# Interleaving two tokens instead of four in the one-hot matrices of a gate product

## The chip, the cores and the metric

The kernel runs on one core of one Trainium2 chip. The metric is the device time of one execution in microseconds (us). The profile tells of five engines: PE (TensorE, matrix products; PEld is its weight load, which runs beside the products), DVE (VectorE), ACT (ScalarE), POOL (GpSimd) and SP (SyncE, which here only issues DMAs).

## What is computed

The reference runs two transformer layers one after the other over 512 tokens of width 1024. The change lies in the last step of the second layer, a product-key mixture of experts ("PEER"): each token picks, in each of 8 heads, 16 of 128 x 128 experts, gives each pick a softmax weight, and sums the picked rows.

```python
idx = jnp.take_along_axis(cand_i, pos, axis=-1)          # i1 * 128 + i2
g = jax.nn.softmax(top_s, axis=-1)
u = down[idx]
act = jax.nn.gelu(jnp.einsum("thkd,td->thk", u, xb).astype(F32), approximate=False)
return jnp.einsum("thk,thkd->td", (g * act).astype(xb.dtype), up[idx])
```

## The kernel before

Each of the 512 tokens has 128 picks (8 heads x 16), each a pair of numbers (i1, i2) and a weight g. The first 128 tokens fetch their expert rows one by one (`gen_fetch`). For the other 384 the kernel takes all 16384 experts densely: scores of every expert for every token (`s_mm`, two halves of 12 matmuls with 384 columns for each of 128 expert blocks), times a gate matrix G[i1, i2] per token that holds the summed weight of each picked expert and zero elsewhere.

The gate matrices are what the change touches. `decode(a)` works out i1, i2 and g of a block of 128 tokens, transposes them on PE so that the partitions are the 128 picks, and stores them in the table `hk_` (i2, i1, the f16 high part of g, the f16 rest of g; four rows of 128 tokens). `gates(a, hook)` then walks over the 128 tokens in groups q of four, two groups at a time, so 16 iterations for each of the blocks a = 1, 2, 3, 48 in all, and 96 groups. For each group DVE makes two instructions of 1024 f16 elements: an equality test of the table against 0..127 (`iota4`), which gives the one-hot rows of i2 and i1 (`oh`), and a product of the i1 one-hot with the two parts of g (`gh`). `gates_mm` then makes 8 matmuls for the group: for each of its 4 tokens, the one-hot of i2 is the stationary and the weighted one-hot of i1 the moving operand, 128 x 128 x 128, once for each part of g, into one PSUM bank. So there are 96 x 8 = 768 such gate matmuls, and 192 such DVE instructions.

Within a group the four tokens are interleaved: element (i, token r) of a one-hot lies at 4 * i + r, so that a token's 128 elements, which a matmul reads, lie four f16 elements, 8 bytes, apart, for both operands.

The order is written out by hand. An iteration issues on DVE: test, test, product, product of two groups. Then `gates_flush` issues the ACT instructions that move the finished banks out (`gates_out`: 512 elements into `b_Gs`, and after eight groups a DMA to `gscr` and two POOL copies), `gates_mm` issues the 16 matmuls of the pair of groups made one iteration before, and `hook` (`ghook`) issues one half of an expert score (`sp(1)`: 12 matmuls, `s_mm`), pending weight-split work on DVE and ACT, and in iterations 5 to 9 one fetched row on DVE. The one-hot buffers are four (`b_oh`, turned by `ohr`), so DVE can be two pairs of groups ahead of PE. Scores are made ahead for 56 of the 128 expert blocks (`NPRE`): what is not made beside the gates is made right after them, and then comes the main loop of `NGR * KT` = 128 steps, to the end of the kernel.

Of the kernel before, what the change touches and what calls it, by code (L numbers as in the profile page):

```python
# [13 lines left out]
ALU = mybir.AluOpType  # L14
AX = mybir.AxisListType.X
MUL, ADD, SUB = ALU.mult, ALU.add, ALU.subtract

P = 128
# [3 lines left out]
NT = 4  # L22
# [10 lines left out]
GW = 32768.0  # L33
# [184 lines left out]
def build(tc, A, cst, coff, uoff, out, stop=None, dbg=None):  # L218
# [8 lines left out]
    V, S, G, PE, SP = nc.vector, nc.scalar, nc.gpsimd, nc.tensor, nc.sync  # L227
# [5 lines left out]
    def al(n, top=False):  # L233
        n = max(8, -(-n // 8) * 8)
        for i in (range(len(holes) - 1, -1, -1) if top else range(len(holes))):
            o, m = holes[i]
            if m >= n:
                if top:
                    holes[i] = (o, m - n)
                    b = Buf(arena[:, o + m - n:o + m], o + m - n, n)  # L240
                else:
                    holes[i] = (o + n, m - n)
                    b = Buf(arena[:, o:o + n], o, n)
                if holes[i][1] == 0:
                    holes.pop(i)
                return b
        raise MemoryError(f"arena: {n} wanted, {holes}")
# [30 lines left out]
    def mm(o, l, r, start=True, stop=True):  # L278
        PE.matmul(o, l, r, start=start, stop=stop)  # L279

    def tr(o, i):
        PE.transpose(o, i, (ident if i.dtype == F32 else ident16)[:i.shape[0], :i.shape[0]])  # L282
# [9 lines left out]
    def act(o, i, f=AF.Copy, **kw):  # L292
        S.activation(o, i, f, **kw)  # L293
# [10 lines left out]
    def stt(o, a, s, b, op0, op1):  # L304
        V.scalar_tensor_tensor(o, a, s, b, op0=op0, op1=op1)  # L305

    def tt(o, a, b, op, e=None):
        (e or V).tensor_tensor(o, a, b, op=op)  # L308
# [81 lines left out]
    def need(key):  # L390
        while key not in ready:
            before = len(ready)
            pump_split(1)
            assert len(ready) > before, (key, q_split[:3], len(spl_free), len(stg_free), list(staged))
        return ready[key]
# [31 lines left out]
    def wk(b, nk, ncol, c0, n=P):  # L427
        h, l = b.h(nk, ncol), b.h(nk, ncol, at=2048)
        return [(h[:, k, c0:c0 + n], l[:, k, c0:c0 + n]) for k in range(nk)]
# [3 lines left out]
    ident, ones, iota = small(P), small(P), small(P)  # L433
# [543 lines left out]
    for a in range(2):  # L977
        b = tbk()
# [7 lines left out]
    for a in range(NT):  # L986
        b, b2 = tbk(), tbk()
# [442 lines left out]
    for a, _ in enumerate(tokproj("rv", hx, range(NT), to_act(rv))):  # L1430
# [4 lines left out]
        else:  # L1435
            d = a - 2
            b = sb_()
# [64 lines left out]
    b = sb_()  # L1502
# [8 lines left out]
    for i in range(2):  # L1511
        b = tb()
# [6 lines left out]
    for i in range(6):  # L1519
        b = lbk()  # L1520
# [75 lines left out]
    w = need(("in", 8))  # L1596
    for p in range(2):
        b = pb()
# [170 lines left out]
    for n in range(KT):  # L1769
        w = wk(need(("wout", n // 2)), KT, 256, P * (n % 2))  # L1770
        b = pb()
# [100 lines left out]
    def sp(n=1):  # L1872
        for _ in range(n):
            if se[2] < NPRE:
                pieces[se[3] % 2]()
                se[3] += 1
# [62 lines left out]
    for h in range(8):  # L1939
        w = need(("wq", h))  # L1940
# [27 lines left out]
        for aa in range(2):  # L1968
            b = gbk()
# [29 lines left out]

    b_g, b_i, b_if = al(NT * P), al(NT * P), al(NV // 2)  # L2000
    gw, i12, If = b_g.f(NT, 16, 8), b_i.h(2, NT, P), b_if.h(NT, 2, 16, 8)
    b_mx, b_pf, b_ij, b_i4 = al(NT * 8), [al(256) for _ in range(4)], al(1024), al(256)
    mx = b_mx.f(NT * 8)
    ts_ = b_TS.f(NT * 8, 16)
    pos, pa, pb_, pt_ = (b.h(NT * P) for b in b_pf)
    iotaj, iota4 = b_ij.h(16, P), b_i4.h(P, 4)
    G.tensor_copy(iotaj, iota[:, 0:16].unsqueeze(2).to_broadcast([P, 16, P]))
    G.tensor_copy(iota4, iota.unsqueeze(2).to_broadcast([P, P, 4]))
    V.tensor_copy(pos.rearrange("p (a k h) -> p a k h", a=NT, k=16), PO.rearrange("p a h k -> p a k h"))
    V.tensor_copy(mx, ts_[:, :, 0])  # L2010
    tt(ts_, ts_, mx.unsqueeze(2).to_broadcast([P, NT * 8, 16]), SUB)
# [24 lines left out]
    b_eq, b_ix, b_hk = al(1024), al(P + EX), [al(4 * 64) for _ in range(2)]  # L2036
# [4 lines left out]
    def decode(a):  # L2041
        for i, ps_ in enumerate((pa, pb_)):
            x_ = ps_[:, P * a:P * a + P].unsqueeze(1)
            tt(eq, iotaj, x_.to_broadcast([P, 16, P]), ALU.is_equal)
            sp(PRE[2])
            eq4 = b_eq.h(16, 16, 8)
            tt(eq4, eq4, If[:, a, i].unsqueeze(2).to_broadcast([P, 16, 16, 8]), MUL)
            for n in (8, 4, 2):
                tt(eq[:, 0:n], eq[:, 0:n], eq[:, n:2 * n], ADD)
            sp(PRE[2])  # L2050
            tt(i12[:, i, a], eq[:, 0], eq[:, 1], ADD)
        if a < 2:
            t = tmps[a][:, 0:P]
            stt(t, i12[:, 0, a], 128.0, i12[:, 1, a], MUL, ADD)
            V.tensor_copy(ix[0] if a == 0 else ix1, t)
        if a:
            hk_ = b_hk[a % 2].h(4, P)
            b = gbk()
            b16 = b.bitcast(F16)
            for i in range(2):  # L2060
                tr(b16[:, P * i:P * i + P], i12[:, 1 - i, a])
            tr(b[:, 256:256 + P], gw[:, a].rearrange("p k h -> p (k h)"))
            act(hk_[:, 0:2], b16[:, 0:256].rearrange("p (i t) -> p i t", i=2))
            act(hk_[:, 2], b[:, 256:256 + P], scale=GW)
            stt(hk_[:, 3], b[:, 256:256 + P], GW, hk_[:, 2], MUL, SUB)


    gscr = drp.tile([NB, P, P - GE, 32], F32, name="gscr")
# [14 lines left out]
    def gates_flush():  # L2083
        while gpend:
            gates_out(*gpend.pop(0))

    def gates(a, hook):
        hk_ = b_hk[a % 2].h(4, P)
        for q0_ in range(EX // 4 if a == 1 else 0, 32, 2):
            two = []  # L2090
            bc = lambda q, i: hk_[:, i:i + 2, 4 * q:4 * q + 4].unsqueeze(2).to_broadcast([P, 2, P, 4])
            for q in (q0_, q0_ + 1):
                b_ = ohr()
                oh, gh = b_.h(2, P, 4), b_.h(2, P, 4, at=8 * P)
                tt(oh, iota4.unsqueeze(1).to_broadcast([P, 2, P, 4]), bc(q, 0), ALU.is_equal)
                two.append((q, oh, gh))
            for q, oh, gh in two:
                tt(gh, oh[:, 1:2].to_broadcast([P, 2, P, 4]), bc(q, 2), MUL)
            gates_flush()
            gates_mm()  # L2100
            gmm.extend((P * a + 4 * q - T0, oh, gh) for q, oh, gh in two)
            hook()

    def gates_mm():
        while gmm:
            t_, oh, gh = gmm.pop(0)
            b = gbk()
            for r_ in range(4):
                for i in range(2):
                    mm(b[:, P * r_:P * r_ + P], oh[:, 0, :, r_], gh[:, i, :, r_], i == 0, i == 1)  # L2110
            gpend.append((b, t_ // 32, t_ % 32 // 4))


# [58 lines left out]
    def ghook():  # L2172
# [5 lines left out]
        if gcnt[0] % 3 == 0:  # L2178
            pump_hi()

    decode(0)
    acc_init(0)
    decode(1)
    if EX:
        spread()
    gates(1, ghook)
    gates_flush()
    if EX:
# [5 lines left out]
    for a in (2, 3):  # L2194
        decode(a)
        if a == 3:
            fr(b_i, b_eq, b_if, b_ij, *b_pf)
            ring(spl_free, 8 - len(ready), 1024)
        gates(a, ghook)
        gates_flush()  # L2200
    gates_mm()
    sp()
    gates_flush()
# [111 lines left out]
    for gr in range(NGR):  # L2315
# [4 lines left out]
        for k in range(KT):  # L2320
# [3 lines left out]
            b = gbk()  # L2324
            ws = []
            for e in range(GE):
                u = us[e // 4]
# [63 lines left out]
```

## Time and profile before

| | us |
|---|---|
| median of 3 runs | 2744.43 (2741.17 to 2744.72) |
| profiled execution, its own time | 2744.41 |
| span of the profiled execution | 2742.6 |
| PE busy | 2650.7 (97%) |
| DVE busy | 2052.6 (75%) |
| ACT busy | 1033.0 (38%) |

The span runs from the first to the last instruction of the program; the rest of the execution's time, 1.8 us, lies around it. Shares of busy time are means over stages with different limits, and a PE that is called busy need not be at its peak, since the matmuls overlap and their ends are modelled. So the stage in question is read by itself. Line numbers are those of the instruction's issue: a helper such as `mm` (L279), `tr` (L282), `act` (L293), `stt` (L305) or `tt` (L308) records all its uses under its own line, so they are told apart by shape and time.

### The profile page before, as it was taken

What the parts mean: (1) busy time and instruction counts of PE and PEld (TensorE: products, weight loads), DVE (VectorE), ACT (ScalarE), POOL (GpSimd) and SP (SyncE); (2) the same over time, 40 slices, a digit from 0 to 9 for tenths busy, and PEclk for the clock granted to TensorE, in tenths of its full rate; (3) what the DMA queues carried; (4) which work ended last, traced back from release to release, by engine and by line L of the source; (5) the groups of instructions that cost most, each with busy time, mean ns of one, the idle gap of its engine ahead of it and who ended that gap; (6) DMA issues with size and microseconds to landing.
All of it is one profiled execution on the core that took longest, in us unless ns stands there. A gap on an engine that the chain in (4) does not pass through costs nothing.

```text
span 2742.6 us, 43709 instructions
## 1 busy us (share of the span) xinstructions
PE 2650.7 (97%) x17395; PEld 1698.6 (62%) x17395; DVE 2052.6 (75%) x3641; ACT 1033.0 (38%) x1634; POOL 436.6 (16%) x602
## 2 busy tenths in 40 slices
PE   7999999999899999999999899999999999999998
PEld 4666666685565444588777555777666666666665
DVE  6898548867776886675535899877699777787785
ACT  3444312245655534543533542334333222222224
POOL 1000000001120000011012132100123333333320
PEclk9999999999999999999999999999999999999999
DMA  6688438422017796934212795766999999999982
GB/s 264 246 331 331 180 134 303 156 94 76 32 47 267 280 330 229 333 110 144 72 47 69 260 340 178 262 221 248 353 368 380 366 349 353 352 343 345 359 301 91
DMA packets 209522, 654.53 MB, mean 239 GB/s; under 512 B 18946, under 2 KB 85284, under 8 KB 188836
## 3 DMA queue, kind: packets, MB, share of 16 engines
q1 hardware_dynamic: 156900, 451.90, 45.1%
q0 software_dynamic: 44352, 188.76, 19.7%
q10 hardware_dynamic: 8064, 11.06, 1.1%
q8 instruction: 136, 2.23, 0.3%
q14 instruction: 70, 0.57, 0.1%
HBM read 549.02 MB, written 102.63 MB: 238 GB/s over the span
## 4 chain that ended last, share of the span: by engine, by line
PE 80%; DVE 13%; ACT 3%; issue 2%; POOL 1%; DMA 0%; ACTq 0%; SPq 0%; DVEq 0%; POOLq 0%
PE psum L279 79%; DVE arena L305 7%; ACT arena L293 3%; DVE arena L308 2%; PE psum L282 2%; DVE arena L1898 1%; DVE arena L1895 1%; POOL arena L308 1%; DVE arena L1902 1%; ACT L293 0%; DVE arena L495 0%; DVE arena L1087 0%; DMA arena<-in_vecs_dram 0%; DMA arena<-in_down_t_dram 0%; DVE arena L1533 0%
## 5 line engine op out<-in xcount | busy, mean ns | idle before, releaser
L279 PE MATMUL psum<-arena 128*128 128x384 f16 (+8 forms) x16840 | 2601.0, 317 | 57.2 <-ACT arena L293 27.8
L279 PEld LDWEIGHTS <-arena 128*128 128x128 f16 x16116 | 1547.9, 99 | 931.6 <-issue 31.1
L305 DVE SCALAR_TENSOR_TENSOR arena<-arena 128x1024 f16<-128x1024 f32 (+6 forms) x1277 | 1096.0, 894 | 161.0 <-ACT arena L293 137.3
L293 ACT ACTIVATE arena<-arena 128x1024 f16<-128x1024 f32 (+9 forms) x993 | 705.8, 752 | 1220.6 <-DVE arena L305 936.8
L308 DVE TENSOR_TENSOR arena<-arena 128x1024 f16<-128x1024 f16 (+11 forms) x668 | 381.8, 590 | 145.6 <-ACT arena L293 102.0
L293 ACT ACTIVATE arena<-psum 128x512 f32<-128x512 f32 (+7 forms) x522 | 267.5, 527 | 458.4 <-PE psum L279 397.4
L305 DVE SCALAR_TENSOR_TENSOR arena<-psum,arena 128x384 f32<-128x384 f32 (+4 forms) x293 | 171.9, 590 | 238.2 <-PE psum L279 205.6
L308 POOL TENSOR_TENSOR arena<-arena 128x256 f32<-128x256 f32 (+7 forms) x249 | 123.3, 518 | 793.5 <-ACT arena L293 247.7
L2142 POOL DMA_INDIRECT arena<-in_peer_down_dram,arena x128 | 132.0, 1031 | 291.0 <-DVE arena L2148 265.1
L2142 POOL DMA_INDIRECT arena<-in_peer_up_dram,arena x128 | 126.2, 986 | 240.5 <-DVE arena L305 227.7
L2148 DVE SCALAR_TENSOR_TENSOR arena<-arena 128x1024 f32<-128x1024 f32 x128 | 156.1, 1220 | 0.3 <-DMA arena<-in_peer_down_dram,arena 0.2
L279 PEld LDWEIGHTS psum<-arena 128*128 128x128 f32 (+1 forms) x724 | 95.2, 186 | 60.8 <-ACT arena L293 19.7
L425 POOL DMA_DIRECT2D arena<-in_units_dram x52 | 27.7, 533 | 647.1 <-DVE arena L305 641.8
L282 PE MATMUL psum<-arena 128*128 128x128 f32 (+2 forms) x555 | 77.8, 271 | 26.9 <-DVE arena L308 13.4
L282 PEld LDWEIGHTS psum<-arena 128*128 128x128 f32 (+1 forms) x493 | 57.6, 142 | 35.2 <-DVE arena L308 13.6
L308 DVE TENSOR_TENSOR arena<-psum,arena 128x384 f16<-128x384 f32 (+3 forms) x95 | 52.3, 579 | 16.9 <-ACT arena L293 9.2
L1898 DVE FIND_INDEX8 arena<-arena 128x8 uint32<-128x128 f32 (+1 forms) x192 | 47.5, 260 | 0.0
L1895 DVE MAX8 arena<-arena 128x8 f32<-128x128 f32 (+1 forms) x192 | 42.3, 256 | 4.5 <-POOL arena L308 4.2
L293 ACT ACTIVATE arena<-psum,arena 128x768 f32<-128x768 f32 (+4 forms) x54 | 39.6, 735 | 15.9 <-PE psum L279 10.0
L2081 POOL COPY arena<-arena 128x128 f32<-128x128 f32 x24 | 16.0, 694 | 181.3 <-ACT arena L293 178.2
L293 ACT ACT_TABLE_LOAD x29 | 37.2, 1283 | 10.4 <-PE psum L279 7.9
L1087 DVE TENSOR_REDUCE arena<-psum 128x1 f32<-128x768 f32 x32 | 30.4, 950 | 7.4 <-PE psum L279 7.3
(54 smaller groups left out, 212.3 us busy)
## 6 DMA issues: line engine op xcount, KB each, us to landing
arena<-in_units_dram SPq DMA_DIRECT2D x91, 1024.0 KB, 7.0
arena<-dscr SPq DMA_DIRECT2D x128, 512.0 KB, 6.2
arena<-in_units_dram SPq DMA_DIRECT2D x128, 512.0 KB, 7.9
arena<-in_down_t_dram SPq DMA_DIRECT2D x118, 512.0 KB, 7.8
dscr<-arena SPq DMA_DIRECT2D x118, 512.0 KB, 6.9
arena<-in_units_dram POOLq DMA_DIRECT2D x52, 1024.0 KB, 6.2
gscr<-arena SPq DMA_DIRECT2D x12, 1920.0 KB, 7.4
arena<-gscr SPq DMA_DIRECT2D x30, 768.0 KB, 9.7
```

The costliest lines, as they stand in the source:

```text
L279: PE.matmul(o, l, r, start=start, stop=stop)
L282: PE.transpose(o, i, (ident if i.dtype == F32 else ident16)[:i.shape[0], :i.shape[0]])
L293: S.activation(o, i, f, **kw)
L305: V.scalar_tensor_tensor(o, a, s, b, op0=op0, op1=op1)
L308: (e or V).tensor_tensor(o, a, b, op=op)
L425: q_raw.append((key, lambda b: eng.dma_start(b.f(n), src)))
L1087: V.tensor_reduce(n[:, 0:1], s_, axis=mybir.AxisListType.XY, op=ALU.max, negate=True)
L1895: V.max(v[:, c_], x)
L1898: V.max_index(i[:, c_], v[:, c_], x)
L1902: V.match_replace(x, v[:, c_], x, NEG)
L2142: G.indirect_dma_start(out=held[job].f(D), out_offset=None, in_=W["peer_up_2" if job[0] else "peer_down_2"], in_offset=bass.IndirectOffset ...
L2148: V.scalar_tensor_tensor(row, row, 1.0, acc, op0=MUL, op1=MUL, accum_out=c_[:, j:j + 1])
```

## The change

A group still holds four tokens, but as two pairs. Its test and its product are laid out as (pair, row, 128, token of the pair), so a token's 128 elements lie two f16 elements, 4 bytes, apart instead of four. The table `hk_` is stored to match: for each pair of tokens the two index rows, and the two weight rows, of two adjacent tokens each. The numbers of instructions, their element counts, the buffers and the order of issue stay. `iota4` (512 elements per partition) becomes `iota2` (256).

```diff
-    iotaj, iota4 = b_ij.h(16, P), b_i4.h(P, 4)
+    iotaj, iota2 = b_ij.h(16, P), b_i4.h(P, 2)
-    G.tensor_copy(iota4, iota.unsqueeze(2).to_broadcast([P, P, 4]))
+    G.tensor_copy(iota2, iota.unsqueeze(2).to_broadcast([P, P, 2]))
...
-            hk_ = b_hk[a % 2].h(4, P)
+            hk_ = b_hk[a % 2].h(2, 64, 2, 2).rearrange("p w u i t -> p w i u t")
...
-            act(hk_[:, 0:2], b16[:, 0:256].rearrange("p (i t) -> p i t", i=2))
-            act(hk_[:, 2], b[:, 256:256 + P], scale=GW)
-            stt(hk_[:, 3], b[:, 256:256 + P], GW, hk_[:, 2], MUL, SUB)
+            w_ = b[:, 256:256 + P].rearrange("p (u t) -> p u t", t=2)
+            act(hk_[:, 0], b16[:, 0:256].rearrange("p (i u t) -> p i u t", i=2, t=2))
+            act(hk_[:, 1, 0], w_, scale=GW)
+            stt(hk_[:, 1, 1], w_, GW, hk_[:, 1, 0], MUL, SUB)
...
-            bc = lambda q, i: hk_[:, i:i + 2, 4 * q:4 * q + 4].unsqueeze(2).to_broadcast([P, 2, P, 4])
+            bc = lambda q, w: hk_[:, w, 4 * q:4 * q + 4].unsqueeze(2).to_broadcast([P, 4, P, 2])
...
-                oh, gh = b_.h(2, P, 4), b_.h(2, P, 4, at=8 * P)
-                tt(oh, iota4.unsqueeze(1).to_broadcast([P, 2, P, 4]), bc(q, 0), ALU.is_equal)
+                oh, gh = b_.h(2, 2, P, 2), b_.h(2, 2, P, 2, at=8 * P)
+                tt(b_.h(4, P, 2), iota2.unsqueeze(1).to_broadcast([P, 4, P, 2]), bc(q, 0), ALU.is_equal)
...
-                tt(gh, oh[:, 1:2].to_broadcast([P, 2, P, 4]), bc(q, 2), MUL)
+                tt(gh, oh[:, :, 1:2].to_broadcast([P, 2, 2, P, 2]),
+                   hk_[:, 1, 4 * q:4 * q + 4].rearrange("p (u i) t -> p u i t", i=2).unsqueeze(3).to_broadcast([P, 2, 2, P, 2]), MUL)
...
-                    mm(b[:, P * r_:P * r_ + P], oh[:, 0, :, r_], gh[:, i, :, r_], i == 0, i == 1)
+                    mm(b[:, P * r_:P * r_ + P], oh[:, r_ // 2, 0, :, r_ % 2], gh[:, r_ // 2, i, :, r_ % 2], i == 0, i == 1)
```

## Rows read from the trace of the kernel before

**Rows 1.** The page, part 1: busy us, share of the span, instructions.
```profile
PE 2650.7 (97%) x17395; PEld 1698.6 (62%) x17395; DVE 2052.6 (75%) x3641; ACT 1033.0 (38%) x1634; POOL 436.6 (16%) x602
```

**Rows 2.** Busy time by stage: gates of each block, decodes between, and what follows.
```profile
core 0: us, PE busy (x) PEld busy (x) DVE busy (x) ACT busy (x) POOL busy (x), PEclk, DMA share, GB/s
1725.90:1781.60 55.70, 54.82 (x400) 43.24 (x399) 48.48 (x77) 22.10 (x38) 9.25 (x10) 1.00 0.70 263
1781.60:1794.40 12.80, 12.80 (x89) 8.87 (x88) 8.37 (x14) 2.96 (x7) 0.00 (x0) 1.00 0.39 119
1794.40:1851.00 56.60, 56.60 (x414) 44.78 (x413) 41.34 (x65) 21.47 (x38) 5.97 (x8) 1.00 0.67 240
1851.00:1863.80 12.80, 12.80 (x89) 8.88 (x88) 8.38 (x14) 2.95 (x7) 0.00 (x0) 1.00 0.41 120
1863.80:1920.50 56.70, 56.70 (x416) 44.89 (x414) 46.66 (x71) 26.88 (x44) 5.32 (x8) 1.00 0.76 278
1920.50:1926.00 5.50, 5.50 (x45) 4.69 (x43) 1.14 (x2) 2.29 (x4) 0.00 (x0) 1.00 0.38 124
1926.00:1981.50 55.50, 54.70 (x338) 32.78 (x336) 37.39 (x64) 18.40 (x29) 10.86 (x13) 1.00 1.04 374
```

**Rows 3.** Timeline of one gate iteration: start us, us, engine, instructions [idle before <-releaser].
```profile
1802.23 0.69 DVE L308 TENSOR_TENSOR arena<-arena 128x1024 f16<-128x1024 f16 x1 [0.33 <-PE psum L279]
1803.17 1.90 DVE L308 TENSOR_TENSOR arena<-arena 128x1024 f16<-128x1024 f16 x3 [0.24 <-PE psum L279]
1806.06 0.69 DVE L308 TENSOR_TENSOR arena<-arena 128x1024 f16<-128x1024 f16 x1 [0.99 <-PE psum L279]
```

**Rows 4.** Gate matmuls and weight loads, 1805.30 to 1806.05: timeline; then min/median/max ns.
```profile
1805.02 1.23 PE L279 MATMUL psum<-arena 128*128 128x128 f16 x9
L279 PE MATMUL psum<-arena x9: 294/296/299, 1805.0 to 1806.0; 128*128 128x128 f16 x9
L279 PEld LDWEIGHTS <-arena x7: 115/115/118, 1805.3 to 1806.0; 128*128 128x128 f16 x7
```

**Rows 5.** The same views of `acc_init`, 1714.52 to 1715.15, whose 16 matmuls read contiguously.
```profile
1714.31 1.06 PE L279 MATMUL psum<-arena 128*128 128x128 f16 x16
L279 PE MATMUL psum<-arena x16: 219/219/219, 1714.3 to 1715.1; 128*128 128x128 f16 x16
L279 PEld LDWEIGHTS <-arena x13: 97/98/98, 1714.5 to 1715.1; 128*128 128x128 f16 x13
```

**Rows 6.** Timeline of score matmuls, 1803.50 to 1804.75, and their ns.
```profile
1803.29 1.62 PE L279 MATMUL psum<-arena 128*128 128x384 f16 x9
L279 PE MATMUL psum<-arena x9: 324/326/326, 1803.3 to 1804.6; 128*128 128x384 f16 x9
```

**Rows 7.** All groups of PE by shape: the one with 128 f16 columns.
```profile
L279 PE MATMUL psum<-arena 128*128 128x128 f16 x784 | 99.3, 295 | 0.9 <-DVE arena L308 0.9
```

**Rows 8.** What DVE waited for, 1724 to 1926: us in total, times, longest.
```profile
DVE arena L308 <- PE psum L279: 32.4, 59, 1.0
DVE arena L305 <- ACT arena L293: 8.6, 3, 4.1
```

**Rows 9.** Timeline of DVE around `decode(2)`.
```profile
1779.80 10.35 DVE L308 TENSOR_TENSOR arena<-arena 128x1024 f16<-128x1024 f16 x15 [0.24 <-PE psum L279]
1794.20 0.29 DVE L305 SCALAR_TENSOR_TENSOR arena<-psum,arena 128x128 f16<-128x128 f32 x1 [4.05 <-ACT arena L293]
```

**Rows 10.** Groups of DVE by shape, 1724 to 1926: busy us, mean ns, idle before.
```profile
L308 DVE TENSOR_TENSOR arena<-arena 128x1024 f16<-128x1024 f16 x196 | 126.4, 695 | 32.6 <-PE psum L279 32.4
L305 DVE SCALAR_TENSOR_TENSOR arena<-arena 128x1024 f16<-128x1024 f32 x8 | 9.8, 1230 | 0.0
L308 DVE TENSOR_TENSOR arena<-arena 128x2048 f16<-128x2048 f16 x8 | 9.8, 1223 | 0.2
```

**Rows 11.** Timeline of f32 matmuls in the selection stage, 1651.45 to 1652.25, and their ns.
```profile
1651.19 1.28 PE L279 MATMUL psum<-arena 128*128 128x128 f32 x10
L279 PE MATMUL psum<-arena x10: 275/275/275, 1651.2 to 1652.2; 128*128 128x128 f32 x10
```

**Rows 12.** The chain that ended last, its longest piece after the gates.
```profile
1981.47 667.40 PE psum L279 x4106
```

**Rows 13.** Groups of 1742 to 1927 that fill `hk_`; timeline row of the `iota4` copy.
```profile
L293 ACT ACTIVATE arena<-psum 128x256 f16<-128x256 f16 x2 | 0.8, 383 | 7.3 <-PE psum L282 3.6 <-DMA sscr<-arena 3.6
1691.78 1.00 POOL L2008 CAST arena<-arena 128x512 f16<-128x512 f32 x1
```

More of the change, by code (lines that the diff above doesn't have):

```diff
@@ L2001, in build @@
     gw, i12, If = b_g.f(NT, 16, 8), b_i.h(2, NT, P), b_if.h(NT, 2, 16, 8)
-    b_mx, b_pf, b_ij, b_i4 = al(NT * 8), [al(256) for _ in range(4)], al(1024), al(256)
+    b_mx, b_pf, b_ij, b_i4 = al(NT * 8), [al(256) for _ in range(4)], al(1024), al(128)
     mx = b_mx.f(NT * 8)
@@ L2087, in gates @@
     def gates(a, hook):
-        hk_ = b_hk[a % 2].h(4, P)
+        hk_ = b_hk[a % 2].h(2, P, 2)
         for q0_ in range(EX // 4 if a == 1 else 0, 32, 2):
             two = []
-            bc = lambda q, i: hk_[:, i:i + 2, 4 * q:4 * q + 4].unsqueeze(2).to_broadcast([P, 2, P, 4])
+            bc = lambda q, w: hk_[:, w, 4 * q:4 * q + 4].unsqueeze(2).to_broadcast([P, 4, P, 2])
             for q in (q0_, q0_ + 1):
                 b_ = ohr()
-                oh, gh = b_.h(2, P, 4), b_.h(2, P, 4, at=8 * P)
-                tt(oh, iota4.unsqueeze(1).to_broadcast([P, 2, P, 4]), bc(q, 0), ALU.is_equal)
+                oh, gh = b_.h(2, 2, P, 2), b_.h(2, 2, P, 2, at=8 * P)
+                tt(b_.h(4, P, 2), iota2.unsqueeze(1).to_broadcast([P, 4, P, 2]), bc(q, 0), ALU.is_equal)
                 two.append((q, oh, gh))
             for q, oh, gh in two:
-                tt(gh, oh[:, 1:2].to_broadcast([P, 2, P, 4]), bc(q, 2), MUL)
+                tt(gh, oh[:, :, 1:2].to_broadcast([P, 2, 2, P, 2]),
+                   hk_[:, 1, 4 * q:4 * q + 4].rearrange("p (u i) t -> p u i t", i=2).unsqueeze(3).to_broadcast([P, 2, 2, P, 2]), MUL)
             gates_flush()
```

## The prediction, made before the changed kernel was run

> **What bounds the kernel now.** I read the page's busy shares first: PE is called busy 97% of the span, DVE 75% [rows 1]. Neither says which one the gate stage waits for, so I cut the trace into windows at the gates and decodes [rows 2]. The gates run from 1725.9 to 1926.0, 200.1 us, with PE filled in all windows but the first (0.9 us idle), while DVE is busy for 48.48 + 8.37 + 41.34 + 8.38 + 46.66 + 1.14 = 154.4 us. The view of waits says why DVE idles: 32.4 us for PE before a test, as the one-hot buffer is still being read, and 8.6 us for ACT at the three fillings of `hk_` [rows 8]. The timeline shows the rhythm: the same test starts at 1802.23 and at 1806.06, so an iteration takes 3.83 us, and DVE works for four instructions of it [rows 3]. After the gates PE is filled again and carries the chain for 667.4 us in one piece [rows 12]. So PE sets the gate stage, and time taken from PE there moves everything after it forward, as far as DVE lets it.
>
> Next, what PE does in 3.83 us. Nine gate matmuls cover 1.23 us with a last one of 0.296 us, so they start (1.23 - 0.296) / 8 = 116.8 ns apart [rows 4]. Nine score matmuls of 384 columns: (1.62 - 0.326) / 8 = 161.8 ns [rows 6]. 16 x 116.8 + 12 x 161.8 = 1869 + 1942 = 3811 ns, which is the iteration. The row that makes the case is that of `acc_init`: the same shape and type, each with its own weight load too, but with 128 adjacent elements in both operands. Its 16 start (1.06 - 0.219) / 15 = 56.1 ns apart and last 219 ns, not 296; weight loads 98 ns, not 115 [rows 4, 5]. [...] So a gate matmul costs 60.7 ns more than its shape does. What differs is the 8-byte distance of its elements.
>
> **The change part by part.** *PE.* 768 gate matmuls (784 of the shape less `acc_init`'s 16 [rows 7]) go from 8 to 4 bytes between elements, in both operands. No row shows f16 at 4 bytes. The bounds are the contiguous 56.1 ns (2 bytes) and today's 116.8 ns (8 bytes): between 46.6 us and nothing off PE. A loss is excluded, since more elements lie in any stretch of memory, not fewer. I take 56.1 ns: at 8 bytes, two elements lie in 16 bytes and a matmul takes about twice its contiguous time; if what costs is the fetch of a stretch wider than one 4-byte word, two or more columns now share each fetch and the doubling goes. An iteration would then need 16 x 56.1 + 1942 = 2840 ns of PE.
>
> [...]
>
> *DVE.* 192 tests and products keep 1024 elements. Three of them together cover 1.90 us, the last 0.69, so they start 0.605 us apart, 2.42 us an iteration [rows 3]; below PE's new 2.84. What changes is that the repeated input is read in runs of 2 elements, no longer 4. No row has runs of 2; the rows nearest are runs of 4 (695 ns) and the decode's 2048 elements, half of them with runs of 8 and half of 128 (1223 ns mean) [rows 10]: (1223 - 695) / 1024 = 0.52 ns per element at each. Bounds: no change, or the loss of two elements at a time, as an instruction with an f32 input has, 1230 ns [rows 10]. A gain is excluded as 4 and 128 cost the same. I take no change, by the nearest row (runs of 4).
>
> *Storing the picks.* Three fillings of `hk_`, each of two ACT instructions (the larger 383 ns) and one on DVE (290 ns) [rows 9, 13], write the same elements in runs of 2. Between nothing and twice their time, 3 x 1 us; I take nothing. They stand in DVE's wait for ACT [rows 8], so they are not covered. The `iota2` copy on POOL halves one of 1.00 us that ends 30 us before its first use [rows 13]; worth nothing either way. No queue, wait or DMA is moved.
>
> *The sum.* PE cannot give its whole 46.6 us, as DVE is next late. I take each window's longer engine and add about 1 us where one leads, 2 where they tie [rows 2]. PE loses 256 x 60.7 ns = 15.5 us in each block of gates.
> Block 1: PE 54.8 - 15.5 = 39.3, DVE 48.5 (it has the five fetched rows): 49.5, saves 6.2.
> Block 2: PE 41.1, DVE 41.3: 43.3, saves 13.3.
> Block 3: PE 41.2, DVE 46.7: 47.7, saves 9.0.
> The two decodes, 12.8 each: DVE works 8.4 and waits 4.05 for the fillings [rows 9], whose transposes stand on PE behind what it is late with and four score halves (7.8 us). With PE less late, some 10.9 each: saves 3.8.
> Tail: the last two pairs of groups, 32 x 60.7 ns: 2.0.
> Sum 34.3 us. From the profiled execution's 2744.4 (its span 2742.6 with 1.8 around it; the median is the same 2744.4) that gives 2710.1. The most it can be is DVE's idle time, 32.4 + 8.6 = 41.0 [rows 8]: 2703.
>
> **The rivals.** *No gain.* PE may fetch one 4-byte word per step and use of it what belongs to the column; then 4 bytes apart is as slow as 8. For it: f32 matmuls, whose columns are 4 bytes apart, start (1.28 - 0.275) / 9 = 111.7 ns apart, close to the gates' 116.8 [rows 4, 11]. Against it: f32 differs in its type as well as in the distance, and the rows cannot separate the two. Time: 2744, or 2738 if the gates come down to f32's 111.7 or a little under (768 x 5 to 8 ns). [...]
>
> *Half a gain.* Only one of the two operands gets cheaper, or weight loads and moving reads still collide: 116.8 - 30.4 = 86 ns. PE then needs 47.0, 48.8 and 48.9 us in the blocks, with DVE's 48.5, 41.3 and 46.7: 49.5 each, saving 6.2, 7.1, 7.2, and 3 at decodes and tail. 2744.4 - 23.5 = 2721. The same time comes out if a full gain is partly given back behind the gates, where DMA stands at 1.04 of its engines' time [rows 2] while scores still wait for their loads; PE waits little there today (0.8 us), so I expect no more than 10 us back.
>
> *Slower: DVE loses its pairs.* If a run of 2 makes DVE take one element at a time, each of the 192 costs 1230 - 695 = 535 ns more, 102.7 us. DVE then needs 154.4 + 102.7 = 257.1 us and, with some 6 us of fillings and end, sets the stage at 263 instead of 200.1: 2744 + 63 = 2807, whatever PE gains. It decides from DVE's 41.0 us of slack over 192 instructions, 0.21 us each: above some 0.91 us a test the kernel gets slower. Against it is that runs of 4, 8 and 128 showed no difference [rows 10].
>
> **How the numbers follow.** Full gain 0.54, at 2703 to 2716; half gain or part of it given back 0.12, at 2716 to 2732; no gain 0.25, at 2738 to 2746; slower 0.09, near 2807. The likeliest is 2710. Its case alone leaves 0.46 out and with half a gain 0.34, so the range goes on to no gain: 2703 to 2746. A measurement of this kernel can tell about 0.2%, 5.5 us, from no change. Faster: 0.54 + 0.12 and 0.01 of the no-gain case, 0.67; same 0.24; slower 0.09.
>
> **What would show it.** In the changed kernel's groups the 128-column f16 matmuls should fall from 295 ns to about 220 and their weight loads from 115 to 98; the same test should come back after about 2.84 us; DVE's 32.4 us of waiting for PE should fall to a few us, and PE should wait for DVE instead. The 1024-element tests should stay at 695 ns: near 1230 is the slower rival. Matmuls still near 296 ns are the no-gain rival, 255 half a gain. With short matmuls but a saving under 28 us, my sum by windows is wrong: the two engines take turns more than I allow, or the stage behind the gates gives time back.

## The result: 2709.8 us, and the profile after

The changed kernel takes 2709.77 us (median of 4 runs, 2707.51 to 2710.74), against 2744.57 for the kernel before on the same chip: a ratio of 0.9873, 95% interval [0.9857, 0.9888]. The forecast was 2710. The profiled execution took 2709.16 us, its span 2707.4.

First the gate matmuls of the kernel after, in the views of [rows 4]: a timeline row of PE (start us, us from the first start to the last end), then the minimum, median and maximum ns of one, for matmuls and for weight loads.

```profile
1791.47 1.08 PE L279 MATMUL psum<-arena 128*128 128x128 f16 x16
L279 PE MATMUL psum<-arena x16: 218/218/221, 1791.5 to 1792.3; 128*128 128x128 f16 x16
L279 PEld LDWEIGHTS <-arena x14: 96/97/97, 1791.6 to 1792.3; 128*128 128x128 f16 x14
```

Sixteen of them start (1.08 - 0.218) / 15 = 57.5 ns apart, where it was 116.8 [rows 4], and one lasts as long as the contiguous one of `acc_init` [rows 5]: 218 ns, its weight load 97.

The stages, in the view of [rows 2] (a stretch, then busy us and instructions of each engine, the granted clock, the share of the DMA engines, GB/s). The first six rows answer to the first six there; the last runs from the end of the gates to the start of the main loop, as the last row there does.

```profile
core 0: us, PE busy (x) PEld busy (x) DVE busy (x) ACT busy (x) POOL busy (x), PEclk, DMA share, GB/s
1725.10:1772.10 47.00, 43.26 (x407) 29.83 (x406) 47.00 (x78) 21.22 (x38) 15.10 (x9) 1.00 0.79 298
1772.10:1783.50 11.40, 11.40 (x92) 7.51 (x89) 8.31 (x14) 2.82 (x7) 2.61 (x2) 1.00 0.57 179
1783.50:1826.20 42.70, 42.60 (x413) 30.69 (x411) 39.95 (x66) 20.02 (x38) 8.31 (x8) 1.00 0.85 305
1826.20:1837.70 11.50, 11.50 (x94) 7.61 (x92) 8.19 (x13) 2.80 (x7) 0.00 (x0) 1.00 0.61 183
1837.70:1886.40 48.70, 45.16 (x420) 31.68 (x418) 44.93 (x71) 25.60 (x45) 24.49 (x8) 0.96 0.85 309
1886.40:1889.50 3.10, 3.10 (x36) 2.32 (x34) 1.13 (x1) 1.54 (x3) 0.00 (x0) 1.00 0.98 392
1889.50:1946.20 56.70, 54.62 (x338) 32.69 (x336) 37.21 (x64) 18.77 (x30) 10.89 (x13) 1.00 1.03 370
```

The gate stage is 164.4 us long, not 200.1: 35.7 us less, and the whole span is 35.2 us shorter. What was the full column before, PE, has gaps now in blocks 1 and 3 (43.26 of 47.00 and 45.16 of 48.70 us), while it is still filled in block 2 (42.60 of 42.70) and in the decodes; the full column of block 1 is DVE: 47.00 of 47.00. The waits of DVE over the stage turned with it (us in total, times, longest), and the tests kept their duration (group row: busy us, mean ns, idle before), as against [rows 8, 10]:

```profile
DVE arena L308 <- PE psum L279: 6.5, 10, 2.0
DVE arena L305 <- ACT arena L293: 6.2, 3, 2.9
L308 DVE TENSOR_TENSOR arena<-arena 128x1024 f16<-128x1024 f16 x196 | 121.7, 687 | 6.7 <-PE psum L279 6.5
```

One thing in the windows was not in the forecast: in block 3 DVE works 44.93 us of 48.70, PE 45.16, the granted clock's mean falls to 0.96, and POOL is called busy 24.49 us, where it was 5.32 [rows 2]. It is taken up in the second set of experiments.

### The profile page after: what moved, and what is told of

Same layout as the page of the kernel before. It is cut to its first block, busy times and chain, and to the rows that moved or that the text cites. A ratio compares the mean times of both kernels' runs of the same rounds, so it can differ in the third digit from the quotient of the medians.

```text
span 2707.4 us, 43710 instructions
## 1 busy us (share of the span) xinstructions
PE 2611.2 (96%) x17395; PEld 1654.8 (61%) x17395; DVE 2046.8 (76%) x3641; ACT 1029.1 (38%) x1634; POOL 465.7 (17%) x602
## 4 chain that ended last, share of the span: by engine, by line
PE 77%; DVE 14%; ACT 3%; DMA 2%; issue 2%; POOL 2%; SPq 0%; ACTq 0%; DVEq 0%; POOLq 0%
PE psum L279 75%; DVE arena L305 7%; DVE arena L308 3%; ACT arena L293 3%; PE psum L282 2%; DVE arena L1898 1%; DVE arena L1895 1%; DMA arena<-in_units_dram 1%; POOL arena L308 1%; POOL arena L2083 1%; DVE arena L1902 1%; ACT L293 0%; DVE arena L495 0%; DVE arena L2151 0%; DMA arena<-gscr 0%
## 5 line engine op out<-in xcount | busy, mean ns | idle before, releaser
L279 PE MATMUL psum<-arena 128*128 128x384 f16 (+8 forms) x16840 | 2561.9, 314 | 61.6 <-ACT arena L293 31.1
L279 PEld LDWEIGHTS <-arena 128*128 128x128 f16 x16116 | 1502.4, 98 | 940.1 <-issue 34.2
L282 PEld LDWEIGHTS psum<-arena 128*128 128x128 f32 (+1 forms) x493 | 57.2, 142 | 34.4 <-DVE arena L308 13.9
L2083 POOL COPY arena<-arena 128x128 f32<-128x128 f32 x24 | 46.4, 1962 | 113.9 <-ACT arena L293 113.9
```

Of the source, the lines that this page charges most:

```text
L2083: G.tensor_copy(b_Gt[hf].f(NB, 4, 32)[:, nb], Gs[:, 4 * hf:4 * hf + 4])
```

## Experiments on the reading of PE

The forecast said that the distance between a token's elements costs PE its time, and left three things open: whether it is that alone, which operand it is, and by what rule. Four kernels, and a fifth after them, keep everything else of the changed kernel, DVE's instructions too, and let PE read other addresses of the same one-hot buffers. With `L` and `R` for the two views, the edit is

```diff
-                    mm(b[:, P * r_:P * r_ + P], oh[:, r_ // 2, 0, :, r_ % 2], gh[:, r_ // 2, i, :, r_ % 2], i == 0, i == 1)
+                    mm(b[:, P * r_:P * r_ + P], L, R, i == 0, i == 1)
+    # 8 bytes:  L = b_.h(P, 4)[:, :, r_]       R = b_.h(2, P, 4, at=8 * P)[:, i, :, r_]
+    # 16 bytes: L = b_.h(P, 8)[:, :, r_]       R = b_.h(P, 8, at=8 * P)[:, :, 4 * i + r_]
+    # 6 bytes:  L = b_.h(P, 3)[:, :, r_ % 3]   R = b_.h(P, 3, at=8 * P + 512 * i)[:, :, r_ % 3]
```

**Both operands at 8 bytes again.**

> The changed kernel with DVE's new layout, table and instructions, but PE reads both operands of a gate matmul at a distance of 8 bytes again, from the same buffers. It multiplies other elements than the reference does, so the gate matrices differ from it; nothing else is left out. Theory (the whole gain is PE's reading): gate matmuls start 117 ns apart and last about 296 ns, the 1024-element tests stay at 0.60 us apart, and the time is that of the kernel before, 2744 (2738 to 2748). Rival (part of the gain came from DVE's side or the smaller table): below 2735 with the same 117 ns.

Measured 2742.63 us (ratio to the kernel before 1.0001 [0.999, 1.0012]).

```profile
1791.70 1.95 PE L279 MATMUL psum<-arena 128*128 128x128 f16 x15
L279 PE MATMUL psum<-arena x15: 296/296/299, 1791.7 to 1793.3; 128*128 128x128 f16 x15
```

(1.95 - 0.296) / 14 = 118.1 ns, and the time of the kernel before. The gate stage itself, here and below taken from the start of the first test to the issue of the last store of gates (`gscr`), shows it more sharply than the whole time; first this run, then the kernel before, in the view of the stages:

```profile
1724.08:1925.11 201.03, 200.15 (x1447) 155.93 (x1446) 154.35 (x237) 79.36 (x137) 20.78 (x26) 1.00 0.67 238
1725.89:1926.90 201.01, 200.13 (x1447) 155.93 (x1446) 154.38 (x237) 79.26 (x137) 20.55 (x26) 1.00 0.66 239
```

201.03 and 201.01 us. DVE's new layout, the table and the smaller `iota2` give nothing by themselves: the gain is PE's reading.

**The stationary operand at 4 bytes, the moving one at 8; and the other half.**

> As the run with both at 8 bytes, but the stationary operand is read at 4 bytes and only the moving one at 8 (the gate matrices differ from the reference's). If the moving read sets the pace: about 107 ns between gate matmuls (117 without the collision with a slow weight load), weight loads back to 98 ns, time 2735 to 2742. If the weight load set it: 56 ns and about 2710.

Measured 2741.90 us (0.9996 [0.9984, 1.0007]); the rows of PE and of its weight load:

```profile
1793.87 1.93 PE L279 MATMUL psum<-arena 128*128 128x128 f16 x15
L279 PE MATMUL psum<-arena x15: 294/297/300, 1793.9 to 1795.5; 128*128 128x128 f16 x15
L279 PEld LDWEIGHTS <-arena x14: 115/116/119, 1794.0 to 1795.5; 128*128 128x128 f16 x14
```

> The other half: moving operand read at 4 bytes, stationary at 8 (the gate matrices differ from the reference's). If the moving read sets the pace: 56 to 60 ns between gate matmuls although the weight loads may stay near 115 ns, time about 2710. If the weight load set it: about 107 ns and 2735 to 2742.

Measured 2706.92 us (0.9871 [0.9842, 0.99]):

```profile
1792.33 1.05 PE L279 MATMUL psum<-arena 128*128 128x128 f16 x15
L279 PE MATMUL psum<-arena x15: 218/222/223, 1792.3 to 1793.2; 128*128 128x128 f16 x15
L279 PEld LDWEIGHTS <-arena x13: 96/113/114, 1792.4 to 1793.2; 128*128 128x128 f16 x13
```

The moving operand alone sets the pace: with it at 8 bytes, (1.93 - 0.297) / 14 = 116.6 ns whatever the weights do; with it at 4 bytes, (1.05 - 0.222) / 14 = 59.1 ns although the weights lie 8 bytes apart and their loads last 113 ns. Two details of the expectations fell. I had put 10 of the 117 ns down to a collision with a slow weight load; with weights at 4 bytes they stay. And weight loads do not show their own cost: they last 116 ns with weights at 4 bytes, beside a slow moving read. On PE's side half of the change, the interleaving of `gh`, is worth all of it here.

**Both at 16 bytes, and both at 6.** These ask for the rule.

> Both operands read at a distance of 16 bytes (the gate matrices differ from the reference's). Theory A (what costs is each 16-byte stretch that a read touches, about 1.67 ns or the time of four columns; that explains 56 ns at 2 and 4 bytes and 107 plus a collision at 8): 128 stretches give 213 ns or a little more between gate matmuls, so PE needs 768 x 100 ns = 77 us more than in the kernel before, time 2810 to 2830. Theory B (columns are read two at a time where both lie in the same 8 bytes, else one at a time, at 107 ns for 128): still about 117 ns and 2744.

Measured 2879.84 us (1.0502 [1.0471, 1.0532]); under it the rows of the run at 6 bytes.

```profile
1791.07 3.91 PE L279 MATMUL psum<-arena 128*128 128x128 f16 x16
L279 PE MATMUL psum<-arena x16: 393/414/419, 1791.1 to 1794.6; 128*128 128x128 f16 x16
```

> Both operands read at a distance of 6 bytes (the gate matrices differ from the reference's). The runs at 8 and 16 bytes gave 117 and 233 ns, that is 1.82 ns for each 16-byte stretch. Theory A (every stretch costs 1.82 ns, whatever the distance): 128 x 6 / 16 = 48 stretches give 87 ns, time near 2721. Theory B (full speed needs a distance that puts four columns evenly into 16 bytes; any other distance over 4 bytes goes at half speed): 117 ns and 2742. Theory C (half speed begins only at 8 bytes): 56 to 60 ns and 2709.

Measured 2715.45 us in a single execution (beside 2744.42 for the kernel before); the third row is its gate stage:

```profile
1793.15 1.56 PE L279 MATMUL psum<-arena 128*128 128x128 f16 x16
L279 PE MATMUL psum<-arena x16: 248/252/254, 1793.2 to 1794.5; 128*128 128x128 f16 x16
1719.48:1897.30 177.82, 176.94 (x1447) 133.38 (x1446) 152.33 (x237) 77.38 (x137) 23.39 (x26) 1.00 0.74 268
```

At 16 bytes (3.91 - 0.41) / 15 = 233 ns, at 6 bytes (1.56 - 0.252) / 15 = 87.2 ns. Put in one line, with the 16-byte stretches that 128 columns touch:

| distance, bytes | 2 | 4 | 6 | 8 | 16 |
|---|---|---|---|---|---|
| stretches of 16 bytes | 16 | 32 | 48 | 64 | 128 |
| ns between matmuls | 56.1 | 57.5 | 87.2 | 118.1 | 233 |
| ns per stretch | 3.5 | 1.80 | 1.82 | 1.85 | 1.82 |

From 4 bytes on, the time is about 1.82 ns for each stretch, theory A. Of the rivals for 6 bytes, B (half speed for anything uneven) and C (half speed only from 8 bytes) both miss 87 ns, and the B of the run at 16 bytes, another theory, misses 233. That 16 bytes take twice the time of 8, 233 against 118 ns, shows that a stretch, if one is paid for as a whole, is not narrower than 16 bytes. A wider one is not excluded: no run went beyond 16 bytes, and up to there the time just follows the length of memory that is touched. At 2 bytes the 128 columns themselves need longer than 16 stretches would (the score matmuls need 161.8 ns for 384 columns [rows 6], 54 ns for 128). So 4 bytes is the largest distance that is still nearly free here, 57.5 ns against 56.1, and the change took exactly that step. The gate stage at 6 bytes, 177.8 us, is 23.2 us shorter than before and filled by PE; 768 x (117 - 87.2) ns are 22.9 us. The time at 16 bytes lies above the expected 2810 to 2830, for two reasons. The price per stretch was put at 1.67 ns, an estimate (four columns of a score matmul take 161.8 / 96 = 1.69 ns [rows 6]), and is 1.82: 768 x (233 - 117) ns = 89 us of PE in place of 77. And PE lost its clock. The window behind one such row of gate matmuls, in the view of the stages, the matmuls in it, and under them the whole gate stage:

```profile
1800.50:1804.00 3.50, 3.50 (x13) 1.70 (x12) 1.99 (x3) 0.60 (x1) 1.48 (x2) 0.53 0.67 266
L279 PE MATMUL psum<-arena x13: 370/524/524, 1800.3 to 1803.9; 128*128 128x384 f16 x12, 128*128 128x128 f16 x1
1722.58:2061.87 339.29, 338.41 (x1447) 194.76 (x1446) 155.75 (x237) 79.83 (x137) 22.30 (x26) 0.82 0.40 142
```

PE is filled throughout, yet the granted clock is 0.53, and a score matmul lasts 524 ns, not 326 [rows 6]; what PE did before the clock fell was to read at 16 bytes, without a gap (busy for 4.50 of the 4.50 us before the window, at a granted clock of 1.00). Over the whole gate stage the mean is 0.82, and this is the likely place of the other 46 us of the 135 by which the kernel is slower; no run separates it.

## Experiments on what comes next: DVE, and POOL behind it

**One token at a time.** This is the slower rival of the prediction put on the chip: runs of one on DVE, contiguous reads on PE.

> One token at a time: a token's 128 elements lie side by side, so PE reads both operands contiguously, and the table's values are repeated 128 times along the innermost dimension of DVE's tests and products, in runs of one. The result is the reference's. Theory (the slower rival of the prediction, at the one run length that the change avoids): DVE takes one element at a time, each of the 192 instructions lasts about 1.22 us instead of 0.69, DVE sets the gate stage, time 2790 to 2820 although the gate matmuls stay at 56 ns. Rival (DVE keeps two at a time with a repeated single value too): 690 ns and 2708.

```diff
-                tt(b_.h(4, P, 2), iota2.unsqueeze(1).to_broadcast([P, 4, P, 2]), bc(q, 0), ALU.is_equal)
+                tt(b_.h(8, P), iota1.unsqueeze(1).to_broadcast([P, 8, P]), bc(q, 0), ALU.is_equal)
...
-                    mm(b[:, P * r_:P * r_ + P], oh[:, r_ // 2, 0, :, r_ % 2], gh[:, r_ // 2, i, :, r_ % 2], i == 0, i == 1)
+                    mm(b[:, P * r_:P * r_ + P], oh[:, r_, 0], gh[:, r_, i], i == 0, i == 1)
```

Here `bc` gives the 8 table values of a group, each repeated 128 times along the innermost dimension. Measured 2797.78 us (1.0196 [1.0177, 1.0215]). The group of DVE over the gate stage:

```profile
L308 DVE TENSOR_TENSOR arena<-arena 128x1024 f16<-128x1024 f16 x193 | 219.7, 1207 | 4.4 <-PE psum L279 4.2
```

1207 ns, not 687: with runs of one an instruction of 1024 elements takes 0.5 ns an element longer, with runs of two it does not. So of one, two and four tokens, two is the one interleaving in which both engines keep their short times (DVE 687 ns, with one 1207; PE 57.5 ns, with four 116.8 [rows 4]), and the prediction's price for the rival (1230 ns, 2807 us) was near; only its condition, runs of two, did not hold.

**The copies that POOL could not make.** In block 3 of the changed kernel the timeline reads (start us, us, engine, instructions [idle before <-what ended it]):

```profile
1851.10 21.24 POOL L2083 COPY arena<-arena 128x128 f32<-128x128 f32 x4 [9.40 <-ACT arena L293]
1870.79 0.68 DVE L308 TENSOR_TENSOR arena<-arena 128x1024 f16<-128x1024 f16 x1
1871.89 1.47 ACT L293 ACTIVATE arena<-psum 128x512 f32<-128x512 f32 x3 [8.44 <-POOL arena L2083]
1872.54 1.90 PE L279 MATMUL psum<-arena 128*128 128x128 f16 x18 [3.46 <-ACT arena L293]
1873.20 1.33 DVE L308 TENSOR_TENSOR arena<-arena 128x1024 f16<-128x1024 f16 x2 [1.74 <-PE psum L279]
```

and the copies' own line, in the kernel after and, under it, in the kernel before (minimum, median, maximum ns):

```profile
L2083 POOL COPY arena<-arena x24: 292/747/20526, 1738.0 to 1891.1; 128x128 f32<-128x128 f32 x24
```

```profile
L2081 POOL COPY arena<-arena x24: 293/747/824, 1742.1 to 1927.2; 128x128 f32<-128x128 f32 x24
```

A POOL copy of 0.7 us, the first of the four, lasted 20.5 us while DVE ran 32 instructions with two inputs without a gap (29 of them tests and products of the gates; 20.37 of 20.40 us busy in the row below), and ended at 1871.63, just after DVE first idled, at 1871.47 (1870.79 + 0.68).

```profile
1851.10:1871.50 20.40, 17.98 (x173) 12.89 (x172) 20.37 (x32) 7.22 (x12) 20.40 (x1) 1.00 0.93 353
```

Behind it stood ACT, which may not overwrite the buffer that is being copied, for 8.44 us; behind ACT stood PE, for 3.46 us, for want of a free bank; and DVE for PE. In the 4.3 us after that idle PE's granted clock was 0.60 in the mean:

```profile
1872.50:1876.80 4.30, 4.26 (x27) 2.59 (x27) 2.53 (x4) 2.93 (x6) 0.00 (x0) 0.60 0.38 147
```

The rows show that the copy did not end before the row of 32 DVE instructions did, but 0.16 us after it (1871.63 - 1871.47); by what path the one holds up the other they do not show. Two tests: the copies on ACT, in the kernel after and in the kernel before.

> The changed kernel with the 24 copies into the gate buffer (128 f32 each) on ACT instead of POOL. In the changed kernel POOL's copies stretched from 0.7 us to 2 us in the mean, four of them to 21 us together, ACT waited 8.4 us for them once, PE 3.5 us for ACT, and PE's clock fell behind that wait. Theory (POOL is held off while DVE runs its two-input instructions without gaps, and that costs the changed kernel some 5 us): 2703 to 2706. Rival (the wait is covered by the scores that PE makes after the gates, or ACT's 24 x 0.3 us more take its place): 2708 to 2712.

```diff
-                G.tensor_copy(b_Gt[hf].f(NB, 4, 32)[:, nb], Gs[:, 4 * hf:4 * hf + 4])
+                act(b_Gt[hf].f(NB, 4, 32)[:, nb], Gs[:, 4 * hf:4 * hf + 4])
```

> The kernel before (four tokens interleaved) with its 24 copies on ACT instead of POOL. Theory (POOL is held off only once DVE has no more gaps; in the kernel before, DVE waits for PE in every iteration and the copies last 0.7 us): no change, 2740 to 2746. Rival (copies on POOL cost in themselves, and the gain of the run with ACT copies has nothing to do with the change): 2734 to 2738.

With the copies on ACT the changed kernel took 2701.34 us (2695.89 to 2705.90; ratio to the kernel before 0.9845 [0.983, 0.986]), below both ranges expected, and the kernel before 2741.68 (0.9997 [0.9987, 1.0007]). The changed kernel run again beside the second gave 2707.05, ratio 0.9868 [0.9851, 0.9885], an interval that still overlaps that of the copies on ACT, by 0.0009.

The gate stages say it without that doubt. What varies between executions lies for the most part ahead of the gates, where these edits change nothing: the first test starts anywhere from 1719.5 to 1730.0 us. The stage itself repeats: here are the changed kernel, the same in a second execution, the changed kernel with the copies on ACT, and the kernel before with the copies on ACT.

```profile
1725.10:1890.78 165.68, 158.30 (x1449) 110.41 (x1448) 149.52 (x237) 75.09 (x137) 50.52 (x26) 0.99 0.80 288
1729.97:1895.64 165.67, 158.30 (x1449) 110.46 (x1448) 149.57 (x237) 75.11 (x137) 50.52 (x26) 0.99 0.80 287
1725.78:1885.40 159.62, 156.14 (x1449) 109.81 (x1448) 148.02 (x237) 80.38 (x159) 6.69 (x6) 1.00 0.83 302
1721.37:1922.39 201.02, 200.14 (x1447) 155.91 (x1446) 152.73 (x237) 84.90 (x159) 8.10 (x7) 1.00 0.69 246
```

The edit takes 6.1 us off the gate stage after the change and nothing before it (201.02 against 201.01): POOL's copies became a cost through the change, since DVE had lost its gaps. That it is the gaps and not the new layout shows in the run with both operands of PE at 8 bytes: DVE's instructions are those of the changed kernel, its gaps are back, and no copy lasts longer than 828 ns.

```profile
L2083 POOL COPY arena<-arena x24: 293/747/828, 1740.3 to 1925.4; 128x128 f32<-128x128 f32 x24
```

**DVE's five fetched rows.**

> The same, and no fetched row is worked on beside the gates: their five, 1.22 us of DVE each, go to the main loop, where DVE has some 20% of idle time. Theory (DVE is what the gates of the first block now wait for; PE idles 3.7 us there): another 3 us, 2700 to 2703. Rival (the rows cost the same in the main loop, or the later start of their loads does): no better than the copies on ACT alone.

```diff
-NTR, GF = 2, 10
+NTR, GF = 2, 5
```

> The changed kernel with the copies left on POOL, and only the five fetched rows moved from the gates to the main loop. Theory (the 7 us that this edit gave on top of the copies on ACT are DVE time of the first block, and do not depend on the copies): 2701 to 2705. Rival (fewer gaps of DVE hold POOL off all the more, so that without the copies on ACT the gain is lost again): 2707 to 2715.

On top of the copies on ACT: 2694.32 us (2693.45 to 2696.68), ratio 0.9821 [0.9808, 0.9835], the fastest kernel of the study, 0.5% under the changed one and below the 2700 to 2703 expected. Without them: 2704.05, ratio 0.9861 [0.9845, 0.9878], inside the 2701 to 2705 of the theory, but not to be told from the changed kernel's 2707.05 beside it. The gate stages, first with the copies on ACT, then without; the third row is the first run from its first gate matmul to the end of the gates:

```profile
1721.74:1877.47 155.73, 154.85 (x1449) 110.14 (x1448) 142.65 (x227) 79.95 (x159) 1.02 (x2) 1.00 0.82 292
1723.92:1885.19 161.27, 155.35 (x1449) 110.22 (x1448) 143.76 (x227) 74.23 (x137) 52.97 (x22) 1.00 0.79 281
1723.67:1876.20 152.53, 152.53 (x1435) 108.86 (x1435) 140.72 (x223) 78.73 (x156) 0.06 (x1) 1.00 0.82 294
```

With both edits PE has not a gap left from its first gate matmul on. And at the gates the two edits all but add up, as the theory had it: the rows give 3.9 us with the copies on ACT (159.62 to 155.73) and 4.4 without (165.67 to 161.27). The rival's wait is there too; ACT waited longer for POOL's copies without the rows, 19.9 us in all, than in the changed kernel, 11.2:

```profile
ACT arena L293 <- POOL arena L2083: 19.9, 5, 8.4
```

```profile
ACT arena L293 <- POOL arena L2083: 11.2, 3, 8.4
```

It did not take the gain of the gates back. What the second run lost, it lost behind them: from the end of the stage to the end of the span it needs 819.4 us (2704.6 - 1885.19), where the changed kernel again needs 815.9 (2711.5 - 1895.64). Why is open; with the copies on ACT it is 814.2 with and without the rows.

## Why the prediction was right

**What bounds the gates**, right: PE did, by the time between its matmuls, and the gain came from that, as the run with both operands at 8 bytes shows (a gate stage of 201.03 us, 201.01 before).

**The price of a gate matmul**, right: 56.1 ns were taken, 57.5 measured, and all of it from the one row that had the same shape with adjacent elements [rows 5]. The reason given, an if about a stretch wider than one 4-byte word, fits the runs: 57.5 ns at 4 bytes and 118 at 8, and 233 at 16, by which such a stretch would be at least 16 bytes. The prediction gave it 0.54, and no row of before could decide it. It counted both operands; it is the moving one alone. By the elements of the moving operand that lie in 16 bytes, the runs give 118 ns at two, 87 at 2.7 in the mean, and 57.5 only at four.

**DVE unchanged**, right: 687 ns a test, 695 before.

**The sum**, right in its total, 34.3 against 35.7 us at the gates, with errors of up to 2.5 us in its parts, and by luck in part:

| | predicted, us | measured | saving predicted | measured |
|---|---|---|---|---|
| block 1 | 49.5 | 47.0 | 6.2 | 8.7 |
| block 2 | 43.3 | 42.7 | 13.3 | 13.9 |
| block 3 | 47.7 | 48.7 | 9.0 | 8.0 |
| two decodes | 21.8 | 22.9 | 3.8 | 2.7 |
| tail | 3.5 | 3.1 | 2.0 | 2.4 |

Block 1 is DVE's busy time and nothing else: no allowance for taking turns was needed, and DVE itself was 1.5 us shorter than before. Block 3 would have been 44.3 us; so long it is with the copies on ACT, in the row below, filled on PE and on DVE. The wait for POOL ate what the sum had in hand.

```profile
1837.88:1882.16 44.28, 44.28 (x428) 31.75 (x426) 44.28 (x71) 28.43 (x54) 0.00 (x0) 1.00 0.93 347
```

The prediction named no such wait: it said that no queue, wait or DMA is moved, and did not ask what a DVE without gaps does to POOL's copies (20.5 us for one of 0.7). Its total came out because two errors met. With the copies on ACT the gate stage is 41.4 us shorter than before (201.01 - 159.62), some 7 us more than the 34.3 put: of these, 4 are the allowances for taking turns in the blocks, and DVE was busy 149.5 us over the stage, not 154.4. POOL, put at nothing, took 6.1 us back.

**Behind the gates** the sum held as well: from their end to the start of the main loop it is 56.7 us, against 55.5 [rows 2], so 1.2 us came back there, well inside the 10 that were allowed. Another 0.8 us was won ahead of the gates, which the change does not touch (1725.1 against 1725.9), so that agreement to 0.3 us with 2710 is closer than the working can claim.

**The rivals.** No gain fell with the 57.5 ns. f32's 111.7 ns at 4 bytes [rows 11] were therefore not the price of the distance; what they are the price of was not tried. The slower rival was right in its price and wrong in its condition. Half a gain fell in its condition too: making one operand cheaper gives nothing (2741.90 us) or everything (2706.92). Its price has a case in fact, 6 bytes: 87.2 ns where 86 were put, and a gate stage shorter by 23.2 us where 23.5 were put. That its single execution took 2715 us, not 2721, comes from ahead of the gates: its first test starts at 1719.5 us, that of the kernel before at 1725.9.

## What to carry to other kernels

Compare the time between matmuls with that of a row of the same shape that reads adjacent elements; where it is longer, look at the distance of the moving operand's elements first (here 59.1 ns with it at 4 bytes and the stationary one at 8, 116.6 the other way round), and price it by the 16-byte stretches it touches (1.82 ns each here, tried from 4 to 16 bytes). Layouts have two readers: here runs of two f16 elements kept DVE's instruction at 687 ns (1207 with runs of one), and the 4 bytes that go with them kept PE's matmuls 57.5 ns apart (56.1 with adjacent elements [rows 5]). When an engine loses its gaps, ask who lived in them: here POOL's copies did, and an engine with time to spare, ACT, made them at no cost that shows (a gate stage of 159.62 us, not 165.68). And where the change is worth a few microseconds of thousands, compare the stage that it touches before the whole time: the gate stage repeated to 0.1 us, the time to several.

## What was not expected of the hardware

Reading the moving operand cost 1.82 ns per 16 bytes touched (233 ns at 16 bytes' distance, 118 at 8, 87 at 6), and the distance in the stationary operand next to nothing (59.1 ns at 8 bytes, 57.5 at 4). A POOL copy of 0.7 us lasted 20.5 us under an unbroken row of two-input DVE instructions. After 3.5 us of idle PE's granted clock was 0.60 over the next 4.3 us; and it fell to 0.53 without any idle behind matmuls that read their moving operand at 16 bytes (in the kernel before, at 8 bytes, it stayed at 1.00 [rows 2]).
